# Gathers written evenly over the V part, gate loads and a weight load pinned on the load queue, one U chunk behind the first dense block's transposes

## The chip, the cores and the metric

One core of a Trainium2 chip. The metric is device microseconds (us) of one execution. Times within the execution are counted from the first instruction.

## The reference, cut to what matters

One decoder block on 512 positions of width 1024. A mixer (windowed attention beside gated linear attention) comes first; the change does not touch it. Then the channel mixer, with 16384 experts, of which each of 8 heads picks 16 per position:

```python
def block(args):
    xb, eb, gb = args
    ub = jnp.take(u, eb, axis=0)
    hid = jax.nn.gelu(jnp.einsum('tkd,td->tk', ub, xb), approximate=False) * gb
    vb = jnp.take(v, eb, axis=0)
    return jnp.einsum('tk,tkd->td', hid, vb)
...
x = x + gate2 * peer_ffn(h2, peer_wq[l], peer_subkeys[l], peer_u[l], peer_v[l])
...
return rms_norm(x, final_norm_w)
```

## The kernel before, in words

The positions are four blocks of 128. Three of them (`DENSE`, 384 positions) go through **all** experts as dense products; the fourth (`GB` = 3) gathers just the rows it picked.

*Dense path.* The experts are 128 chunks of 128. `u_part(c)` (L687) loads a pair of chunks of U (1 MB, three buffers `raw`), splits a chunk into a high part (ScalarE, L59) and a low part (VectorE or GpSimd, L60), multiplies it with the positions in 24 matmuls of 384 columns (L64 to L66), and applies GELU (ScalarE, L699). Even chunks (`AHEAD`) are computed early and stored to DRAM (`gsp`, L701); odd ones stay in SBUF. The gates of a dense block are made as one-hot products: `route(n)` (L779) finds experts and gates on VectorE in four steps, `gate_transposes(n)` (L836) transposes the two index tiles on TensorE (L841), copies them by ScalarE (L842) and splits the gates into three bf16 parts (L848 to L851), and `gate_group` (L854) builds one-hot tiles on VectorE (L862, L867), multiplies them on TensorE (L874), copies the result (L876) and writes 1 MB of gates to DRAM (`Gd`, L878), 24 times. `v_part(c)` (L1008) loads a pair of chunks of V (L1012), every eighth chunk a piece of the gates (`gr`, L1015, 12 KB a partition, two buffers), multiplies GELU by gates (L1024), splits both into high and low parts (L1028, L1029, L60), and `v_matmuls` adds 18 matmuls of 512 columns into six accumulators.

*Gather path.* `gather_u(s)` (L885) fetches 128 rows of U (0.5 MB) by an indirect DMA that GpSimd issues, and VectorE reduces them with the positions (L889); every eighth step ScalarE and VectorE make eight columns of the hidden values (L892, L893). `gather_v(s)` (L895) fetches rows of V and VectorE adds them to `gacc` (L902). All use a ring `gr` of five buffers, which the one-hot tiles `o12` use before.

*What orders the work.* The framework orders each engine's queue, and SP's queue of loads, when it builds the program: it plays the program through in a simulated run and issues on each engine what is ready, and among what is ready what was written first (`schedule_with_timeline_sim`, L38). Within the stretch from L977 to L994, VectorE and GpSimd keep the written order among the instructions written there; GpSimd does so to the end. On the chip each queue is then in order.

*Order as written.* The steps are `route(3)`, `route(0)`, the transposes of block 0, its gate groups, then blocks 1 and 2. Between steps `u_ahead` (L707) writes U parts: at step k of the first eight it has written up to `WQ_U + (ROUTE_U - WQ_U) * k // 8`, that is 12 to 19 of the 64 even chunks; the 19th is chunk 36. After these steps come the odd chunks 1, 3, 5, 7, and the V loop (L1064): for chunk c the U part of chunk c + 9 (even c), `v_part(c)`, its matmuls, then `gather_to` (L1068), which brings the gathers written so far to 8 + 2 (c + 1). The list of gathers has 18 of U, then V and U by turns. `fwb`, the last norm's weight (0.5 MB over all partitions, L1070), is written after chunk 16.

Of the kernel before, what the change touches and what calls it, by code (L numbers as in the profile page):

```python
# [1 line left out]

# [5 lines left out]
F32 = mybir.dt.float32  # L8
# [9 lines left out]
P = 128  # L18
D = 1024
KD = 8  # L20
# [8 lines left out]
TD = 128 * len(DENSE)  # L29
GB = 3  # L30
TG = 16
NGRP = TD // TG


AHEAD = tuple(range(0, P, 2))
# [6 lines left out]
def peer_block_kernel(ctx: ExitStack, tc: tile.TileContext, a: dict, out: bass.AP):  # L42
    nc = tc.nc
# [8 lines left out]
    def raw(shape, name):  # L52
        return st.tile(shape, F32, tag="raw", bufs=3, name=name)

    def hilo(src, shape, name, lo_eng):
        pool, bufs = ring["hl"]
        hi = pool.tile(shape, FR, tag="hi", bufs=bufs, name=name + "h")
        lo = pool.tile(shape, FR, tag="lo", bufs=bufs, name=name + "l")
        nc.scalar.activation(hi, src, AF.Copy)  # L59
        lo_eng.tensor_tensor(lo, src, hi, OP.subtract)  # L60
        return hi, lo

    def mm3(acc, lh, ll, rh, rl, start, stop):
        nc.tensor.matmul(acc, lh, rh, start=start, stop=False)  # L64
        nc.tensor.matmul(acc, lh, rl, start=False, stop=False)  # L65
        nc.tensor.matmul(acc, ll, rh, start=False, stop=stop)  # L66

    def bcast_load(t, src, n):
        nc.sync.dma_start(t, bass.AP(tensor=src.tensor, offset=src.offset, ap=[[0, P], [1, n]]))

    def rstd_of(pool, ss, n, w, name):
        m = pool.tile([P, w], F32, name=name + "m", tag="rsm", bufs=2)
# [21 lines left out]
    ident = cp.tile([P, P], F32, name="ident")  # L94
# [22 lines left out]
    def bank(name, tag="m"):  # L117
        return banks["pool"].tile([P, 512], F32, tag=tag, bufs=BUFS[tag], name=name)
# [4 lines left out]
    def pbank(name):  # L123
        return ps.tile([P, 512], F32, tag="ph", name=name)
# [485 lines left out]
    h2Th = h2p.tile([P, KD, T], FR, name="h2Th")  # L610
    h2Tl = h2p.tile([P, KD, T], FR, name="h2Tl")
# [72 lines left out]
    gsp = dr.tile([len(AHEAD), P, TD], F32, name="gsp")  # L684
    ges = {}

    def u_part(c, lo_eng=None):  # L687

        j = c // 2 % 2
        if j == 0:  # L690
            u_part.raw[c % 2] = raw([P, 2, KD, P], f"u{c}")
            nc.sync.dma_start(u_part.raw[c % 2], a["uT"][c // 4 + (c % 2) * (P // 4)])
        uh, ul = hilo(u_part.raw[c % 2][:, j], [P, KD, P], f"uc{c}", lo_eng or nc.vector)
        ph = ps.tile([P, 512], F32, tag="ph", name=f"ph{c}")[:, :TD]
        for k in range(KD):
            mm3(ph, uh[:, k, :], ul[:, k, :], h2Th[:, k, :TD], h2Tl[:, k, :TD], k == 0, k == KD - 1)
        ge = dnA.tile([P, NGRP, TG], F32, tag="ge", bufs=RING, name=f"ge{c}")
        gef = ge.rearrange("p g t -> p (g t)")
        nc.scalar.activation(gef, ph, AF.Gelu)  # L699
        if c % 2 == 0:  # L700
            nc.scalar.dma_start(gsp[c // 2], gef)  # L701
        else:
            ges[c] = ge

    u_part.raw = {}

    def u_ahead(upto, lo_eng=None):  # L707
        while u_ahead.n < min(upto, len(AHEAD)):
            u_part(AHEAD[u_ahead.n], lo_eng)
            u_ahead.n += 1  # L710
# [66 lines left out]
    I12 = {}  # L777
# [50 lines left out]
    CG = 8  # L828
    Gd = dr.tile([P // CG, P, NGRP, CG * TG], F32, name="Gd")
# [6 lines left out]
    def gate_transposes(n):  # L836

        t12 = rt.tile([P, P // 2, 2, 2], BF, tag="t12", bufs=2, name=f"t12{n}")
        for s in range(2):
            pt = bank(f"tr{s}{n}", BK[s])  # L840
            nc.tensor.transpose(pt[:, :P], I12[n][:, s], ident)  # L841
            nc.scalar.activation(t12[:, :, s], pt[:, :P].rearrange("p (g r) -> p g r", r=2), AF.Copy)  # L842
        pt = bank(f"trg{n}", BK[2])
        nc.tensor.transpose(pt[:, :P], gates[n], ident)
        gp3 = rt.tile([P, P // 2, 3, 2], BF, tag="gp3", bufs=2, name=f"gp3{n}")
        r = rt.tile([P, P], F32, tag="gr3", bufs=1, name=f"gr3{n}")
        pair = lambda v: v.rearrange("p (g r) -> p g r", r=2)
        nc.scalar.activation(gp3[:, :, 0], pair(pt[:, :P]), AF.Copy)  # L848
        nc.vector.tensor_tensor(pair(r), pair(pt[:, :P]), gp3[:, :, 0], OP.subtract)
        nc.scalar.activation(gp3[:, :, 1], pair(r), AF.Copy)  # L850
        nc.vector.tensor_tensor(gp3[:, :, 2], pair(r), gp3[:, :, 1], OP.subtract)  # L851
        trs[n] = t12, gp3

    def gate_group(bi, n, q):  # L854
        t12, gp3 = trs[n]
# [25 lines left out]
    NS = P  # L881
# [20 lines left out]
            nc.vector.scalar_tensor_tensor(gacc, vr, hg[:, s:s + 1], gacc, op0=OP.mult, op1=OP.add)  # L902


    EARLY, VLAG = 8, 10
    gathers = [(gather_u, s) for s in range(EARLY)]
    rest = [(s * 0.88 / (NS - EARLY), gather_u, s + EARLY) for s in range(NS - EARLY)]
    rest += [((s + VLAG) / (NS + VLAG), gather_v, s) for s in range(NS)]
    gathers += [g[1:] for g in sorted(rest, key=lambda g: g[0])]

    def gather_to(upto):
        while gather_to.n < min(upto, len(gathers)):
            f, s = gathers[gather_to.n]
            f(s)
            gather_to.n += 1
# [30 lines left out]
    WQ_U, ROUTE_U, LAST_U = 11, 19, 5  # L946
# [26 lines left out]
        steps += [lambda n=n: gate_transposes(n)] + grp[:6] + late + grp[6:]  # L973
    NSTEP = 4 * len(DENSE) + 4 + 2 * NGRP
    k = 0
    dve_s = ExitStack()
    dve_s.enter_context(tc.manual_schedule(engines={mybir.EngineType.DVE, mybir.EngineType.Pool}))  # L977
    for g in steps:
        if callable(g):
            g()  # L980
            continue
        for _ in g:
            k += 1
            if k <= 8:
                u_ahead(WQ_U + (ROUTE_U - WQ_U) * k // 8)
            else:
                u_ahead(ROUTE_U + (len(AHEAD) - LAST_U - ROUTE_U) * (k - 8) // (NSTEP - 8))
        if g is steps[0]:
            nc.vector.scalar_tensor_tensor(ix_u, I12[GB][:, 0], 128.0, I12[GB][:, 1], op0=OP.mult, op1=OP.add)
            nc.vector.scalar_tensor_tensor(ix_v, I12[GB][:, 1], 128.0, I12[GB][:, 0], op0=OP.mult, op1=OP.add)  # L990
            nc.vector.tensor_copy(gg_g, gates[GB])
# [8 lines left out]
    dn = ctx.enter_context(tc.tile_pool(name="dn", bufs=1, side="right", reuse_waits="tile"))  # L1000
    pacc = ctx.enter_context(tc.tile_pool(name="pacc", bufs=1, space=PSUM, side="right", reuse_waits="tile"))
    acc = [pacc.tile([P, 512], F32, name=f"acc{i}") for i in range(2 * len(DENSE))]
    fwb = dn.tile([P, D], F32, name="fwb")
    gacc = dn.tile([P, D], F32, name="gacc")
    vPc = a["vP"].rearrange("(c i) d -> c i d", i=P)
    LAST = 4

    def v_part(c):  # L1008
        if c % 2 == 0:

            v_part.raw = dn.tile([P, 2, D], F32, tag="vraw", bufs=2, name=f"v{c}") if c else raw([P, 2, D], "v0")
            nc.sync.dma_start(v_part.raw, vPc[c:c + 2].rearrange("c i d -> i c d"))  # L1012
        if c % CG == 0:
            v_part.g = dn.tile([P, NGRP, CG, TG], F32, tag="gring", bufs=2, name=f"gr{c}")
            nc.sync.dma_start(v_part.g.rearrange("p g c t -> p g (c t)"), Gd[c // CG])  # L1015
        vh, vl = hilo(v_part.raw[:, c % 2], [P, D], f"vc{c}", nc.vector)
        if c % 2 == 0:
            if c % 4 == 0:
                v_part.ge = dnA.tile([P, 2, TD], F32, tag="gel", bufs=2, name=f"gel{c}")
                nc.sync.dma_start(v_part.ge, gsp[c // 2:c // 2 + 2].rearrange("c p t -> p c t"))  # L1020
            ge = v_part.ge[:, c // 2 % 2].rearrange("p (g t) -> p g t", g=NGRP)
        else:
            ge = ges.pop(c)
        nc.vector.tensor_tensor(ge, ge, v_part.g[:, :, c % CG, :], OP.mult)  # L1024
        gef = ge.rearrange("p g t -> p (g t)")
        Ah = dn.tile([P, TD], FR, tag="Ah", bufs=4, name=f"Ah{c}")
        Al = dn.tile([P, TD], FR, tag="Al", bufs=4, name=f"Al{c}")
        nc.scalar.activation(Ah, gef, AF.Copy)  # L1028
        nc.vector.tensor_tensor(Al, gef, Ah, OP.subtract)  # L1029
        return c, Ah, Al, vh, vl  # L1030
# [33 lines left out]
    for c in range(P - LAST):  # L1064
        if c % 2 == 0 and c + 1 + LEAD < P:
            u_part(c + 1 + LEAD)
        v_matmuls([v_part(c)])
        gather_to(EARLY + (len(gathers) - EARLY) * (c + 1) // (P - LAST))  # L1068
        if c == 16:
            bcast_load(fwb, a["fw"], D)  # L1070
        if c == P - 16:

            dg = gp.tile([P, KD, P], F32, tag="gr", bufs=GR, name="dg")
            nc.vector.tensor_tensor(dg, ident[:, None, :].to_broadcast([P, KD, P]),
                                    modT[:, 40:48, None].to_broadcast([P, KD, P]), OP.mult)
            for q in range(2):
                pb = pbank(f"g2b{q}")
                for i in range(4):
                    nc.tensor.matmul(pb[:, i * P:(i + 1) * P], ones, dg[:, 4 * q + i, :], start=True, stop=True)
                nc.scalar.activation(h2n[:, q * 512:(q + 1) * 512], pb, AF.Copy)  # L1080
# [67 lines left out]
```

## Time and profile before

| what | value |
|---|---|
| median of 3 runs | 1559.18 us (1557.12 to 1560.58) |
| the profiled execution | 1555.13 us, its span 1553.4 us |
| granted TensorE clock, mean | 0.990 |
| TensorE busy | 1493.2 us (96%) |
| VectorE busy | 1251.8 us (81%) |
| ScalarE busy | 688.8 us (44%) |
| GpSimd busy | 412.9 us (27%) |
| loads of u, v, gr | 64 of 1024 KB, 64 of 1024 KB, 16 of 1536 KB |
| writes of Gd | 24 of 1024 KB |

The table is the average over stages. A wait is read in the rows below: the number in square brackets behind an instruction is how long its engine was idle before it, and behind the arrow stands what came last of the things that it waited for. An instruction's own time (second column) can overlap the next one's.

### The profile page before, as it was taken

To read this page: it belongs to the slowest core of one execution; us is meant where nothing else is said; L and a number is where in the kernel's file an instruction comes from. 1 tells how busy PE (TensorE), PEld (TensorE's weight loads), DVE (VectorE), ACT (ScalarE), POOL (GpSimd) and SP (SyncE) were. 2 spreads that over 40 slices of the span, in tenths; PEclk is the share of its full clock that TensorE was granted. 3 is DMA by queue.
4 is the path that set the end of the run, shared out by engine and by line. 5 is a ranking of instruction groups with operands and counts; after the bars stand their busy time and mean duration, and the time that the engine had idled before them with its cause. 6 is when DMAs were issued, how large, how long until landed. Compare 5 with 4: busy or idle time off the path is not lost.

```text
span 1553.4 us, 24408 instructions
## 1 busy us (share of the span) xinstructions
PE 1493.2 (96%) x9379; PEld 1328.2 (86%) x9379; DVE 1251.8 (81%) x2476; ACT 688.8 (44%) x1078; POOL 412.9 (27%) x327
## 2 busy tenths in 40 slices
PE   4999989899999999999999999999999999999996
PEld 3787878888998999999888888888888888888885
DVE  7578668589989898995678778878888878887997
ACT  5545576433445666564333333333333333333343
POOL 1000000144500000003243334433434434434550
PEclk9999999999999999999999999999999999999998
DMA  9253444262346677679998999888998989898893
GB/s 349 89 204 131 171 142 173 108 239 92 127 155 188 198 239 235 201 239 388 380 348 317 339 348 346 322 340 333 364 330 329 338 340 354 326 340 334 292 331 129
DMA packets 154932, 409.67 MB, mean 264 GB/s; under 512 B 10288, under 2 KB 77120, under 8 KB 142400
## 3 DMA queue, kind: packets, MB, share of 16 engines
q1 hardware_dynamic: 108736, 261.30, 47.2%
q0 software_dynamic: 36864, 134.23, 23.0%
q10 hardware_dynamic: 9216, 12.59, 2.2%
q8 instruction: 73, 1.20, 0.3%
q14 instruction: 43, 0.35, 0.1%
HBM read 366.14 MB, written 41.94 MB: 263 GB/s over the span
## 4 chain that ended last, share of the span: by engine, by line
PE 63%; DVE 3%; DMA 2%; ACT 1%; issue 1%; DVEq 0%; ACTq 0%; SPq 0%
PE acc L65 11%; PE acc L64 11%; PE acc L66 11%; PE ph L66 8%; PE ph L64 8%; PE ph L65 8%; PE pg L874 4%; DMA Gd<-gs 1%; DMA gr<-Gd 1%; DVE o L867 1%; ACT gs L876 0%; DVE o L862 0%; DVE oh L819 0%; DVE oh L822 0%; DVE oh L817 0%
## 5 line engine op out<-in xcount | busy, mean ns | idle before, releaser
L887 POOL DMA_INDIRECT gu<-in_u_dram,ix_u x128 | 170.2, 1329 | 531.5 <-PE pg L874 273.5
L897 POOL DMA_INDIRECT gv<-in_vP_dram,ix_v x128 | 171.0, 1336 | 214.9 <-DVE gu L889 183.1
L902 DVE SCALAR_TENSOR_TENSOR gacc<-gv,hg,gacc 128x1024 f32<-128x1024 f32 x127 | 162.7, 1281 | 3.3 <-DMA gv<-in_vP_dram,ix_v 3.1
L889 DVE SCALAR_TENSOR_TENSOR gu<-gu,h2n 128x1024 f32<-128x1024 f32 x128 | 156.0, 1219 | 5.9 <-DMA gu<-in_u_dram,ix_u 5.9
L1028 ACT ACTIVATE Ah<-ge 128x384 fp32r<-128x384 f32 x64 | 33.6, 525 | 155.1 <-PE acc L65 155.1
L1028 ACT ACTIVATE Ah<-gel 128x384 fp32r<-128x384 f32 x64 | 33.6, 525 | 154.4 <-PE acc L65 154.4
L876 ACT ACTIVATE gs<-pg 128x512 f32<-128x512 f32 x96 | 94.3, 1108 | 9.8 <-PE pg L874 9.8
L867 DVE TENSOR_TENSOR o<-o,gp 128x1024 bf16<-128x1024 bf16 x144 | 91.0, 687 | 4.3
L874 PE MATMUL pg<-o,o 128*128 128x128 bf16 x1152 | 79.3, 223 | 5.3 <-DVE o L867 5.3
L874 PEld LDWEIGHTS <-o 128*128 128x128 bf16 x1152 | 69.7, 99 | 14.4 <-issue 8.5
L953 POOL IOTA iot<- 128x256 bf16 x1 | 1.5, 1541 | 282.8 <-DVE h2Tl L675 282.8
L1029 DVE TENSOR_TENSOR Al<-gel,Ah 128x384 fp32r<-128x384 f32 x64 | 35.6, 556 | 45.2 <-ACT Ah L1028 45.2
L699 ACT ACTIVATE ge<-ph 128x384 f32<-128x384 f32 x128 | 60.8, 475 | 23.8 <-PE ph L66 23.7
L862 DVE TENSOR_TENSOR o<-iot,t 128x2048 bf16<-128x2048 bf16 x48 | 58.5, 1218 | 4.9 <-ACT t L842 4.9
L1029 DVE TENSOR_TENSOR Al<-ge,Ah 128x384 fp32r<-128x384 f32 x64 | 35.5, 555 | 19.2 <-ACT Ah L1028 18.1
L1024 DVE TENSOR_TENSOR ge<-ge,gr 128x384 f32<-128x384 f32 x64 | 35.4, 553 | 10.9 <-ACT ge L699 10.9
L212 DVE SCALAR_TENSOR_TENSOR macc<-wa,scs,macc 128x1024 f32<-128x1024 f32 x28 | 39.0, 1392 | 4.9 <-DMA wa<-in_w_ada_dram 4.7
L1024 DVE TENSOR_TENSOR gel<-gel,gr 128x384 f32<-128x384 f32 x64 | 32.8, 553 | 0.0
L65 PE MATMUL pq<-h2Tl,wq_0h 128*128 128x512 f32 (+1 forms) x80 | 27.9, 349 | 1.2 <-DVE h2Tl L675 1.2
L64 PE MATMUL pq<-h2Th,wq_0h 128*128 128x512 f32 (+1 forms) x80 | 28.0, 352 | 1.0 <-ACT qha L751 1.0
L65 PE MATMUL pq<-h2Tl,wq_1h 128*128 128x512 f32 (+1 forms) x80 | 28.2, 353 | 0.0
L66 PE MATMUL pq<-h2Th,wq_1l 128*128 128x512 f32 (+1 forms) x80 | 28.2, 352 | 0.0
(2599 smaller groups left out, 5077.1 us busy)
## 6 DMA issues: line engine op xcount, KB each, us to landing
u<-in_uT_dram SPq DMA_DIRECT2D x64, 1024.0 KB
v<-in_vP_dram SPq DMA_DIRECT2D x64, 1024.0 KB
Gd<-gs SPq DMA_DIRECT2D x24, 1024.0 KB
gr<-Gd SPq DMA_DIRECT2D x16, 1536.0 KB
wa<-in_w_ada_dram SPq DMA_DIRECT2D x20, 1024.0 KB
gsp<-ge ACTq DMA_DIRECT2D x64, 192.0 KB
gel<-gsp SPq DMA_DIRECT2D x32, 384.0 KB
wi<-in_w_in_dram SPq DMA_DIRECT2D x9, 1024.0 KB
```

Of the source, the lines that this page charges most:

```text
L64: nc.tensor.matmul(acc, lh, rh, start=start, stop=False)
L65: nc.tensor.matmul(acc, lh, rl, start=False, stop=False)
L66: nc.tensor.matmul(acc, ll, rh, start=False, stop=stop)
L867: nc.vector.tensor_tensor(o2[:, :, m], o12[:, :, 1], gp3[:, g0:g0 + H, m, None].to_broadcast([P, H, P, 2]), OP.mult)
L874: nc.tensor.matmul(pt[:, i, :], o12[:, g, 0, :, r], o2[:, g, m, :, r], start=(m == 0), stop=(m == 2))
L876: nc.scalar.activation(gs[:, :, t0 + 4 * f:t0 + 4 * f + 4].rearrange("p b a -> p a b"), pt, AF.Copy)
L887: nc.gpsimd.indirect_dma_start(out=ur, out_offset=None, in_=a["u"], in_offset=bass.IndirectOffsetOnAxis(ap=ix_u[:, s:s + 1], axis=0))
L889: nc.vector.scalar_tensor_tensor(ur, ur, 1.0, h2n, op0=OP.mult, op1=OP.mult, accum_out=hid[:, s:s + 1])
L897: nc.gpsimd.indirect_dma_start(out=vr, out_offset=None, in_=a["vP"], in_offset=bass.IndirectOffsetOnAxis(ap=ix_v[:, s:s + 1], axis=0))
L902: nc.vector.scalar_tensor_tensor(gacc, vr, hg[:, s:s + 1], gacc, op0=OP.mult, op1=OP.add)
L1024: nc.vector.tensor_tensor(ge, ge, v_part.g[:, :, c % CG, :], OP.mult)
L1029: nc.vector.tensor_tensor(Al, gef, Ah, OP.subtract)
```

## The change

It adds no arithmetic and takes none away. Three things move. (1) The constant `EARLY` goes: the gathers are spread evenly, 256 (c + 1) / 124 written after chunk c, and in the list 11 of U stand first. (2) `gates_of` writes the load of gate piece 0 behind the load of `v0`, and that of piece j + 1 in chunk 8j + 2; these loads and `fwb`'s are pinned: `keep_in_program_order` holds an instruction behind the one written before it on its queue. (3) In the first eight steps `u_ahead` writes up to 11 + 7k // 8 U parts, and the 19th, chunk 36, is written after block 0's transposes; `issue_after` queues its matmuls behind the second index transpose on TensorE.

```diff
-    def u_part(c, lo_eng=None):
+    def u_part(c, lo_eng=None, after=None):
...
-        for k in range(KD):
-            mm3(ph, uh[:, k, :], ul[:, k, :], h2Th[:, k, :TD], h2Tl[:, k, :TD], k == 0, k == KD - 1)
+        with tc.issue_after(after.ins) if after is not None else nullcontext():
+            for k in range(KD):
+                end = mm3(ph, uh[:, k, :], ul[:, k, :], h2Th[:, k, :TD], h2Tl[:, k, :TD], k == 0, k == KD - 1)
...
-            nc.tensor.transpose(pt[:, :P], I12[n][:, s], ident)
+            tr = nc.tensor.transpose(pt[:, :P], I12[n][:, s], ident)
...
-    EARLY, VLAG = 8, 10
-    gathers = [(gather_u, s) for s in range(EARLY)]
-    rest = [(s * 0.88 / (NS - EARLY), gather_u, s + EARLY) for s in range(NS - EARLY)]
-    rest += [((s + VLAG) / (NS + VLAG), gather_v, s) for s in range(NS)]
-    gathers += [g[1:] for g in sorted(rest, key=lambda g: g[0])]
+    VLAG = 10
+    gathers = [(s * 0.88 / NS, gather_u, s) for s in range(NS)]
+    gathers += [((s + VLAG) / (NS + VLAG), gather_v, s) for s in range(NS)]
+    gathers = [g[1:] for g in sorted(gathers, key=lambda g: g[0])]
...
         if callable(g):
-            g()
+            tr = g()
+            if first is None:
+
+                first = u_part(AHEAD[u_ahead.n], after=tr)
+                u_ahead.n += 1
             continue
...
-                u_ahead(WQ_U + (ROUTE_U - WQ_U) * k // 8)
+                u_ahead(WQ_U + (ROUTE_U - 1 - WQ_U) * k // 8)
...
+    def gates_of(j):
+        gates_of.next = dn.tile([P, NGRP, CG, TG], F32, tag="gring", bufs=2, name=f"gr{j}")
+        tc.keep_in_program_order(
+            nc.sync.dma_start(gates_of.next.rearrange("p g c t -> p g (c t)"), Gd[j]))
+
...
+        if c == 0:
+            gates_of(0)
         if c % CG == 0:
-            v_part.g = dn.tile([P, NGRP, CG, TG], F32, tag="gring", bufs=2, name=f"gr{c}")
-            nc.sync.dma_start(v_part.g.rearrange("p g c t -> p g (c t)"), Gd[c // CG])
+            v_part.g = gates_of.next
+        if c % CG == 2 and c + CG < P:
+            gates_of(c // CG + 1)
...
-        gather_to(EARLY + (len(gathers) - EARLY) * (c + 1) // (P - LAST))
+        gather_to(len(gathers) * (c + 1) // (P - LAST))
         if c == 16:
-            bcast_load(fwb, a["fw"], D)
+            tc.keep_in_program_order(bcast_load(fwb, a["fw"], D))
```

## Rows read from the trace of the kernel before

**Rows 1.** Stages: PE, PEld, DVE, ACT, POOL busy (instructions), PEclk, DMA share, GB/s

```profile
470.00:510.00 40.00, 39.77 (x356) 38.21 (x355) 39.10 (x48) 24.91 (x29) 0.00 (x0) 0.94 0.66 203
...
710.00:780.00 70.00, 65.27 (x349) 61.82 (x347) 42.28 (x65) 24.75 (x38) 20.01 (x16) 0.95 0.99 394
...
1200.00:1460.00 260.00, 260.00 (x1256) 228.91 (x1256) 213.55 (x276) 92.80 (x131) 106.75 (x83) 1.00 0.89 333
```

**Rows 2.** Timeline of TensorE: start us, us, engine line op out<-in xcount [idle<-releaser]

```profile
460.62 0.33 PE L64 MATMUL ph<-h2Th,uc36h 128*128 128x384 f32 x1
...
464.61 0.34 PE L66 MATMUL ph<-h2Th,uc36l 128*128 128x384 f32 x1
464.78 0.38 PE L841 MATMUL tr<-ident,I 128*128 128x128 f32 x2
...
468.61 0.37 PE L874 MATMUL pg<-o,o 128*128 128x128 bf16 x2 [1.70 <-DVE o L867]
```

**Rows 3.** Timeline of ScalarE around the transposes

```profile
460.64 1.06 ACT L59 ACTIVATE uc42h<-u 128x1024 fp32r<-128x1024 f32 x1 [2.72 <-PE ph L65]
...
461.98 0.30 ACT L850 ACTIVATE gp<-gr 128x128 bf16<-128x128 f32 x1
...
466.14 0.27 ACT L842 ACTIVATE t<-tr 128x128 bf16<-128x128 f32 x1
```

**Rows 4.** Timeline of VectorE, from block 0's softmax to its first one-hot tile

```profile
443.55 0.40 DVE L787 TENSOR_REDUCE zz<-g 128x8 f32<-128x128 f32 x1 [0.38 <-ACT g L786]
...
444.43 1.22 DVE L60 TENSOR_TENSOR uc30l<-u,uc30h 128x1024 fp32r<-128x1024 f32 x1
...
462.31 0.29 DVE L851 TENSOR_TENSOR gp<-gr,gp 128x128 bf16<-128x128 f32 x1 [2.59 <-ACT gp L850]
...
466.61 1.22 DVE L862 TENSOR_TENSOR o<-iot,t 128x2048 bf16<-128x2048 bf16 x1 [4.00 <-ACT t L842]
```

**Rows 5.** Slices of TensorE: us, PE busy (instructions), PEclk, DMA share, GB/s

```profile
468.00:472.00 4.00, 2.93 (x25) 0.54 0.00 0
472.00:476.00 4.00, 3.77 (x31) 0.61 0.22 45
```

**Rows 6.** Timeline of TensorE from the U part to the V part

```profile
738.75 0.69 PE L64 MATMUL ph<-h2Th,uc1h 128*128 128x384 f32 x1 [2.76 <-ACT ge L699]
...
746.12 0.45 PE L64 MATMUL ph<-h2Th,uc3h 128*128 128x384 f32 x1 [0.17 <-ACT ge L699]
...
764.58 1.65 PE L64 MATMUL acc<-vc0h,Ah 128*128 128x512 f32 x6 [1.52 <-ACT vc0h L59]
766.51 0.50 PE L65 MATMUL acc<-vc0l,Ah 128*128 128x512 f32 x1 [0.28 <-DVE vc0l L60]
```

**Rows 7.** A slice within it, columns as in the stages

```profile
740.00:744.00 4.00, 4.00 (x14) 4.00 (x13) 1.86 (x4) 0.00 (x0) 2.62 (x2) 0.50 1.00 411
```

**Rows 8.** Timeline of ScalarE from the U part to the V part

```profile
737.26 1.06 ACT L59 ACTIVATE uc5h<-u 128x1024 fp32r<-128x1024 f32 x1 [8.20 <-DMA u<-in_uT_dram]
...
744.62 1.06 ACT L59 ACTIVATE uc7h<-u 128x1024 fp32r<-128x1024 f32 x1 [5.93 <-DMA gr<-Gd]
...
763.09 0.49 ACT L699 ACTIVATE ge<-ph 128x384 f32<-128x384 f32 x1 [3.67 <-PE ph L66]
763.48 1.05 ACT L59 ACTIVATE vc0h<-v 128x1024 fp32r<-128x1024 f32 x1
```

**Rows 9.** Timeline of SP's queue of loads: start us, us to issue, what

```profile
713.08 14.39 SPq L692 DMA_DIRECT2D u<-in_uT_dram  x1
...
737.63 0.42 SPq L69 DMA_DIRECT2D fwb<-in_fw_dram  x1
```

**Rows 10.** The chain of waits: start us, us, what

```profile
734.30 9.87 DMA gr<-Gd
744.25 0.33 ACTq L701
```

**Rows 11.** GpSimd's U gathers (L887) alone: stretch, us, busy (count), PEclk, DMA share, GB/s

```profile
690.00:764.00 74.00, 21.61 (x17) 0.95 1.03 387
```

More of the change, by code (lines that the diff above doesn't have):

```diff
@@ L1 @@
-from contextlib import ExitStack
+from contextlib import ExitStack, nullcontext
 import concourse.bass as bass
@@ L65, in mm3 @@
         nc.tensor.matmul(acc, lh, rl, start=False, stop=False)
-        nc.tensor.matmul(acc, ll, rh, start=False, stop=stop)
+        return nc.tensor.matmul(acc, ll, rh, start=False, stop=stop)
     def bcast_load(t, src, n):
-        nc.sync.dma_start(t, bass.AP(tensor=src.tensor, offset=src.offset, ap=[[0, P], [1, n]]))
+        return nc.sync.dma_start(t, bass.AP(tensor=src.tensor, offset=src.offset, ap=[[0, P], [1, n]]))
     def rstd_of(pool, ss, n, w, name):
@@ L703, in u_part @@
             ges[c] = ge
+        return end
     u_part.raw = {}
@@ L852, in gate_transposes @@
         trs[n] = t12, gp3
+        return tr
     def gate_group(bi, n, q):
@@ L975, in peer_block_kernel @@
     k = 0
+    first = None
     dve_s = ExitStack()
```

## The prediction, made blind

> **What bounds the kernel now.** I read the stage table first. From 1200 to 1460 us, deep in the V part, TensorE is busy for 260.00 of 260 us at full clock [rows 1]: nothing done to loads, gathers or VectorE there can gain, and they can only lose. Two stages stand out against that: 470 to 510, with a granted clock of 0.94, and 710 to 780, with 65.27 of 70 us busy, clock 0.95 and a DMA share of 0.99 [rows 1]. The change touches both places, so the sum is made there.
>
> *First place, the start of the first dense block.* TensorE finishes chunk 36's U products at 464.78, and only then runs the two index transposes [rows 2]. ScalarE copies them out at 466.14 [rows 3]. VectorE, which has nothing to do for 4.00 us, starts the first one-hot tile at 466.61 [rows 4], and TensorE, idle for 1.70 us, starts on the first gate products at 468.61 [rows 2]. The clock falls behind that: 0.54 and 0.61 in the two slices from 468 to 476 [rows 5].
>
> *Second place, the passage from the U part to the V part.* TensorE waits 2.76 us for chunk 1's accumulator, runs that chunk's 24 products at half clock (0.50 in 740 to 744), waits 1.52 us for chunk 0's V operand and 0.28 us for its low part [rows 6, 7]. The first wait goes back through ScalarE: chunk 5's high part stands in its queue until 737.26, when its load lands, and the GELU that frees the accumulator stands behind it [rows 8]. That load's issue held SP for 14.39 us [rows 9]. After it the first gate load leaves at 734.30 and takes 9.87 us; the chain goes from its landing to a gsp store on ScalarE's own queue [rows 10], behind which chunk 7's high part has waited 5.93 us [rows 8].
>
> **The change, part by part.**
>
> *1. Chunk 36's U products behind the transposes.* Removed: 24 products ahead of the transposes. They took from 460.62 to 464.78, that is 4.16 us for 24 products, whose first and last are shown [rows 2]. Work moved is 4.16 us, so the gain here cannot exceed 4.2 us. Nothing is added, but eight U parts (chunks 22 to 36) each move one route step later on VectorE, whose order is by hand here.
>
> Whom that makes late: chunk 28's low part now stands behind the softmax of block 0 instead of ahead of it in the tail of route(3). That softmax waits for ScalarE's exponential, so its reduction stays near 443.2 to 443.6 instead of moving up by a whole 1.14 us, and the low part that stood after it started at 444.43 [rows 4]. I get 444.05 for the start and 445.25 for the end. TensorE reaches chunk 28 at 443.8 (four U parts of 4.16 us before 460.62, and some 0.2 us for a transpose among them) and has two products without the low part, 0.35 us: a stall of 1.1 us. The six other low parts up to chunk 34 come out 0.3 to 1.5 us ahead of TensorE by the same count. Their four 1 MB loads have three raw buffers, two pairs of chunks, ahead of use: a step (about 3.5 us) later costs nothing while that cover holds, and up to that step if it is gone.
>
> What is gained: uc42h follows chunk 34's end, now 461.7 instead of 460.64. From there to the second gate copy's end ScalarE took 1.64 us (460.64 to 462.28 [rows 3]), and the two index copies add 0.44 us. The first one-hot can start at 463.8 instead of 466.61: **2.8 us** earlier, which is what VectorE, pacing this stretch, gains. The other end: chunk 36's low part is now written behind the second VectorE step of the transposes, which waited 2.59 us for the gate copy and ran at 462.31 [rows 4]. If ScalarE keeps that order, the low part is ready at 464.85 (1.1 + 462.31 + 0.29, and 1.14), while TensorE has work (transposes, two products) to 462.4: it idles 2.4 us, the clock falls again, and the 1.1 us of stall may be all that is left, as a loss. So -1.1 to 4.2; I take 2.8, since ScalarE's rows give it directly. Nothing in the later blocks changes, and TensorE-bound work carries what is gained to the end.
>
> *2. No gathers ahead (EARLY gone).* Already in the kernel before, no gather is written ahead of chunk 0's V products: the first call stands behind them. Yet 17 are issued by 764 [rows 11]. The planner issues what is ready; fwb, written behind chunk 16, leaves at 737.63 too [rows 9]. Fewer gathers in the early calls do not make any less ready. The number of gathers is the same (256), only 11 instead of 18 U rows now stand ahead of the first V row on POOL's queue, and later ones rank lower against chunks 1 to 4. I cost it at nothing: a gather's VectorE step is about 1.2 us, and the slack that hides eight of them is the V part, where TensorE never waits [rows 1]. Were that cover gone, eight times 1.2 us, 9.8 us, is the most it could cost.
>
> *3. The loads on SP.* gr 0 (1.5 MB) moves behind the load of v0 (1 MB), gr 1 behind v2, gr j+1 behind that of chunk 8j+2, fwb (0.5 MB) behind v16. No instruction is added. Later gate loads have 6 chunks of about 6.2 us in hand and a free buffer by then, so they no longer hold SP; they hid already, so nothing. In the passage the gain is that v0, no longer stuck on SP behind gr 0's wait for Gd, is early in the plan as well, so that its high part is not planned behind chunk 9's GELU: ScalarE sat idle before that GELU, and ran vc0h straight after it at 763.48 [rows 8], so an earlier place costs nothing. That takes away 1.52 and 0.28, **1.8 us** [rows 6]. Bounds: the whole passage costs 2.76 + 0.17 + 1.52 + 0.28 idle and 7.20 - 4.16 = 3.04 us for chunk 1 at half clock, so at most 7.8 gained; on the other side 6.0 lost (the slower rival). I take 1.8, as rows put a cause of order, not of traffic, on just these two waits.
>
> Here a rule weighs in. The rows show gr 0 taking 9.87 us [rows 10], with a U load issued up to 727.47 ahead of it on SP's queue [rows 9]. The Trainium skill, "DMA: Bandwidth & Descriptors", section "Queues, rings and completion order", says that each DMA engine takes turns between queues and works through one queue's ring in order; by that v0 ahead of gr 0 delays the gate load by the whole of v0, which speaks against this pin, and the sum would be the slower rival's instead of mine.
>
> **The sum.** 2.8 + 1.8 = 4.6 us. The profiled execution took 1555.13 us (its span 1553.4), so 1550.5 by its measure; it lies 4.05 us under the median of the runs, 1559.18, and against that median the forecast is **1554.6 us**. A measurement of this kernel can tell about 0.2% from no change, 3.1 us.
>
> **The rivals.**
>
> *The gathers do stay behind* (the change does what its words say). Traffic in 710 to 780 falls from a share of 0.99, chunk 5's load lands in time, and the passage's 7.8 us go with the 2.8: 1559.18 - 10.6 = 1548.6. For it: gathers move 17 rows of 0.5 MB in that stretch, about 8.9 MB. Against: readiness, not program order, decided before. 0.16.
>
> *Nothing to be measured.* The U products shift one wait into another (stall of 1.1 us, ScalarE's order kept, clock falls again), so that about 0.8 us are left, and vc0h keeps its place: 1558.4. For it: VectorE needs the same time for its steps, and two of the three edits move work under a TensorE that is busy anyway. 0.28.
>
> *Slower: the gate load behind v0.* The place is ScalarE's queue at 744: the gsp store waits for gr 0, then chunk 7's high part, the GELU and chunk 3's products. It decides as soon as gr 0 lands later than now, since chunk 1's products end at 745.95 and chunk 3's start at 746.12 [rows 6]. v0 is 1.05 MB; at the passage's 394 GB/s [rows 1] that is 2.7 us, at gr 0's own pace (two thirds of 9.87) 6.6 us. I price it at 4.6, plus 3.0 us of a second spell of half clock, less the 2.8 of part 1, 1.8 not gained: 1559.18 + 4.8 = 1564.0. Against: which store waits for which load depends on the planner's count, and may fall on another load. 0.14.
>
> **How the numbers follow.** The forecast has 0.42. Its own range is 1553.2 (4.2 + 1.8) to 1558.5 (-1.1 + 1.8). The range for 8 in 10 reaches to the first rival below, with a little for its parts, and into the slower one above without its upper half: 1547.5 to 1563. Faster by over 0.2% means under 1556.1: all of the first rival, 0.35 of the forecast's 0.42 and 0.01 of the second, 0.52. Slower: 0.14 and 0.01 for parts that add up badly, 0.15. The rest, 0.33, is the same.
>
> **What would show it.** Part 1: the transposes right behind chunk 34's products, the first one-hot about 3 us earlier against chunk 34's end, a wait of about 1 us at chunk 28, and a clock over 0.9 in the slices after. Part 2: still some 10 or more gathers issued before the first V product; no more than five would mean that the first rival holds. Part 3: v0 ahead of gr 0 on SP, fwb behind v16, vc0h ahead of chunk 9's GELU, no wait at the first V product. I am wrong if the 2.76 us wait and the half clock at chunk 1 vanish, or if chunk 3's products wait for a gate load.

## The result, and the profile after

| kernel | median | runs | range |
|---|---|---|---|
| before, same chip | 1557.07 us | 6 | 1554.99 to 1560.58 |
| changed | 1547.21 us | 6 | 1545.03 to 1554.58 |

The ratio is 0.9941, with a 95% interval from 0.9919 to 0.9962: about 9.2 us faster, where 4.6 were forecast. The changed kernel's profiled execution took 1545.37 us (span 1543.6); 9.76 us lie between it and the one of before.

**The first dense block.** The first two stages of [rows 1], a slice of [rows 5] and that of [rows 7] in the changed kernel:

```profile
470.00:510.00 40.00, 40.00 (x359) 38.64 (x357) 38.73 (x49) 25.61 (x30) 0.00 (x0) 1.00 0.78 241
710.00:780.00 70.00, 68.64 (x371) 65.07 (x371) 44.71 (x61) 25.04 (x37) 18.62 (x16) 1.00 0.98 383
...
472.00:476.00 4.00, 4.00 (x41) 3.84 (x40) 3.90 (x6) 1.83 (x3) 0.00 (x0) 1.00 0.99 342
740.00:744.00 4.00, 4.00 (x25) 4.00 (x24) 2.37 (x3) 1.51 (x3) 1.62 (x2) 1.00 1.05 425
```

Both stages with a clock under 1 are at 1.00 now, and the DMA share of the passage is 0.98, where it was 0.99. TensorE's timeline, to be held against [rows 2]:

```profile
444.55 0.44 PE L66 MATMUL ph<-h2Th,uc28l 128*128 128x384 f32 x1 [0.80 <-DVE uc28l L60]
...
460.98 0.38 PE L843 MATMUL tr<-ident,I 128*128 128x128 f32 x2
461.12 0.42 PE L64 MATMUL ph<-h2Th,uc36h 128*128 128x384 f32 x1
...
465.19 0.33 PE L66 MATMUL ph<-h2Th,uc36l 128*128 128x384 f32 x1
...
465.71 1.62 PE L877 MATMUL pg<-o,o 128*128 128x128 bf16 x24
```

ScalarE and VectorE in the same stretch, against [rows 3, 4]:

```profile
458.68 0.32 ACT L852 ACTIVATE gp<-gr 128x128 bf16<-128x128 f32 x1 [0.40 <-DVE gr L851]
461.00 1.06 ACT L59 ACTIVATE uc42h<-u 128x1024 fp32r<-128x1024 f32 x1 [2.00 <-PE ph L65]
...
462.33 0.27 ACT L844 ACTIVATE t<-tr 128x128 bf16<-128x128 f32 x1
```

```profile
459.03 0.29 DVE L853 TENSOR_TENSOR gp<-gr,gp 128x128 bf16<-128x128 f32 x1 [0.46 <-ACT gp L852]
459.24 1.22 DVE L60 TENSOR_TENSOR uc36l<-u,uc36h 128x1024 fp32r<-128x1024 f32 x1
462.80 1.23 DVE L865 TENSOR_TENSOR o<-iot,t 128x2048 bf16<-128x2048 bf16 x1 [2.35 <-ACT t L844]
```

The transposes stand ahead of chunk 36, the stall at chunk 28 is there (0.80 us; 1.1 forecast), and TensorE goes from chunk 36 to gate products without the 1.70 us wait. The copy that I feared behind uc42h ran ahead of it.

**The passage.** TensorE, then ScalarE, then SP's queue, against [rows 6, 8, 9]:

```profile
733.89 0.44 PE L64 MATMUL ph<-h2Th,uc1h 128*128 128x384 f32 x1 [1.36 <-ACT ge L700]
...
759.22 0.39 PE L64 MATMUL acc<-vc0h,Ah 128*128 128x512 f32 x1
```

```profile
732.41 1.06 ACT L59 ACTIVATE uc5h<-u 128x1024 fp32r<-128x1024 f32 x1 [6.80 <-PE ph L65]
...
736.82 1.06 ACT L59 ACTIVATE uc7h<-u 128x1024 fp32r<-128x1024 f32 x1 [2.98 <-DMA u<-in_uT_dram]
...
739.58 1.06 ACT L59 ACTIVATE uc9h<-u 128x1024 fp32r<-128x1024 f32 x1 [1.32 <-DMA v<-in_vP_dram]
...
748.28 1.06 ACT L59 ACTIVATE vc0h<-v 128x1024 fp32r<-128x1024 f32 x1 [0.85 <-DMA v<-in_vP_dram]
```

```profile
709.80 11.77 SPq L692 DMA_DIRECT2D u<-in_uT_dram  x1
...
723.10 1.52 SPq L1024 DMA_DIRECT2D v<-in_vP_dram  x2
...
732.40 0.37 SPq L1024 DMA_DIRECT2D v<-in_vP_dram  x1
732.87 0.90 SPq L1018 DMA_DIRECT2D gr<-Gd  x2
```

One wait is left. SP sends v2 and v4 at 723.10, right behind the U loads, then v0 at 732.40 and both gate pieces; in the kernel before it stood for 6.2 us (728.08 to 734.27) waiting for the last write of Gd, and all V loads left after that. vc0h runs 11 us ahead of its first use. What I had not forecast is chunk 7's high part: 736.82, not 744.62, and behind a U load, not behind gr 0. GpSimd issues as many gathers up to 764 as before, 19 for 17, 15 of them of U against [rows 11]:

```profile
690.00:764.00 74.00, 20.00 (x15) 1.00 1.03 395
```

**Where the 9.8 us are.** From the starts of the same products in both timelines: 0.76 us ahead of chunk 28 (0.5 of it already at 150 us, where nothing was changed); 4.03 from chunk 28 to chunk 44 (42.38 us before, 38.35 after); 1.55 given back between chunks 80 and 100, where the changed kernel's profile has a spell of half clock; 6.79 from the end of chunk 126 to TensorE's end (805.59 to 798.80); 0.47 given back behind TensorE's end; the rest of the way differs by 0.2.

### The profile page after: what moved, and what is told of

The parts are those of the page before. It is cut to its first block, busy times and chain, and to the rows that moved or that the text cites. A ratio compares the mean times of both kernels' runs of the same rounds, so it can differ in the third digit from the quotient of the medians.

```text
span 1543.6 us, 24413 instructions
## 1 busy us (share of the span) xinstructions
PE 1488.5 (96%) x9379; PEld 1324.5 (86%) x9379; DVE 1250.4 (81%) x2476; ACT 688.4 (45%) x1078; POOL 407.3 (26%) x327
## 4 chain that ended last, share of the span: by engine, by line
PE 65%; DVE 3%; ACT 1%; issue 0%; DMA 0%; DVEq 0%; ACTq 0%
PE acc L65 11%; PE acc L64 11%; PE acc L66 11%; PE ph L64 9%; PE ph L66 9%; PE ph L65 9%; PE pg L877 4%; DVE o L870 1%; ACT gs L879 0%; DVE oh L821 0%; DVE o L865 0%; DVE oh L819 0%; DMA u<-in_uT_dram 0%; DVE y L1063 0%; DVE y L1073 0%
## 5 line engine op out<-in xcount | busy, mean ns | idle before, releaser
L900 POOL DMA_INDIRECT gv<-in_vP_dram,ix_v x128 | 164.7, 1287 | 255.1 <-DVE gu L892 196.8
```

Of the source, the lines that this page charges most:

```text
L900: nc.gpsimd.indirect_dma_start(out=vr, out_offset=None, in_=a["vP"], in_offset=bass.IndirectOffsetOnAxis(ap=ix_v[:, s:s + 1], axis=0))
```

## The experiments

Each kernel was run against the kernel before in five rounds. Intervals are 95%; microseconds are the ratio's distance from 1 times 1557.

### One edit at a time

The U edit alone (`u_part(..., after=tr)`, `ROUTE_U - 1 - WQ_U`):

> Before with the U edit alone. My theory: the first dense block gives 4.8 us, as the changed kernel's trace shows at its second block (first one-hot products 536.38 to 531.58), and the passage to the V part stays as before (waits of 2.76 and 1.52 us, chunk 1 at half clock), since it has its own cause there: 0.9970, that is -4.7 us. Rival (the passage's waits were only a matter of when TensorE arrives): the passage improves too, -8 us or more. Rival (nothing in the first block holds to the end): within 1.5 us of before.

0.9980 [0.9969, 0.9992], 3.1 us faster. From chunk 28 to chunk 44 its profile takes 38.32 us. The passage is not better; from the end of chunk 126 to TensorE's end it takes 1.3 us more than before, with half clock from 747.4 on:

```profile
738.72 0.45 PE L64 MATMUL ph<-h2Th,uc1h 128*128 128x384 f32 x1 [2.27 <-ACT ge L700]
...
746.25 0.44 PE L64 MATMUL ph<-h2Th,uc3h 128*128 128x384 f32 x1 [3.10 <-ACT ge L700]
```

The pins of the gate loads and of `fwb` alone (`gates_of`, two `keep_in_program_order`):

> Before with the gate loads and fwb pinned, U part and gathers as before. My theory: the wait of 1.52 and 0.28 us at the first V product goes (-1.8), and if the 2.76 us wait at chunk 1 shrinks below what lets the clock fall, 3.0 to 4.4 us more: -1.8 to -6.4 us. Rival (the gathers did it): within 1.5 us of before, waits in the passage as before. Slower rival: gr 0 lands later behind v0 and chunk 3's products wait for it: +2.6 to +6.

0.9956 [0.9944, 0.9968], 6.9 us faster, more than the forecast for the whole change. Its passage has one wait, at chunk 1; its first block has the 42 us of before, less a shorter spell of half clock (41.40).

```profile
736.04 0.44 PE L64 MATMUL ph<-h2Th,uc1h 128*128 128x384 f32 x1 [1.71 <-ACT ge L699]
```

The gathers alone (no `EARLY`):

> Before with EARLY gone alone. My theory: readiness decides, some 17 gathers are still issued before the first V product, and the time is within 1.5 us of before. Rival (the gathers did it): fewer than 10 issued by then, DMA share under 0.9 in 710 to 780, -5 to -8 us.

1.0004 [0.9993, 1.0015]: nothing, and 17 gathers up to 764 as before. The three edits add up: 3.1 and 6.9 faster, 0.6 slower make 9.4, and all together measured 9.2. The passage with the gathers alone:

```profile
737.17 0.65 PE L64 MATMUL ph<-h2Th,uc1h 128*128 128x384 f32 x1 [2.24 <-ACT ge L699]
...
744.71 0.44 PE L64 MATMUL ph<-h2Th,uc3h 128*128 128x384 f32 x1 [1.52 <-ACT ge L699]
```

The passages of the U edit and of the gathers tell something that the one of before hid [rows 6]. There chunk 1 ran at half clock and chunk 3 waited for 0.17 us; here chunk 1 runs at full clock, or half of it does, and chunk 3 waits for 3.10 or 1.52. Counted from the end of chunk 126, chunk 3 starts at 10.13 us (before), 9.81 and 9.78. Something other than the clock holds chunk 3: chunk 7's high part, behind gr 0.

### The gathers kept out of the passage

The changed kernel, with the first gather held back:

```diff
-        v_matmuls([v_part(c)])
+        end = v_matmuls([v_part(c)])
+        if c == 0:
+            gather_to.after = end
...
+        if s == 0:
+            tc.add_manual_dep(ins.ins, gather_to.after.ins.name, ...)
```

> The changed kernel with the first gather made to wait for chunk 0's last V product, so that really none runs ahead. What the words of the change promise: DMA share in 700 to 740 falls well under 1, the wait of 1.35 us at chunk 1 goes, up to -1.4 us against the changed kernel and no more, because nothing else is left in the passage; against before 0.993. Rival (18 gathers less ahead cost VectorE time in the V part that it does not have): gathers end later, the last blocks wait for VectorE, slower than the changed kernel by up to 18 x 1.2 = 22 us, less what slack takes; -9.8 + 22 against before at worst.

0.9986 [0.9975, 0.9996], some 7 us slower than the changed kernel. The passage does come clear: no wait at chunk 1, a DMA share of 0.79 from 690 to 764. But the gathers miss at the end. TensorE ends at 1530.85, the last row of V is added then, and the last norm follows behind it (VectorE's timeline):

```profile
1529.17 1.28 DVE L908 SCALAR_TENSOR_TENSOR gacc<-gv,hg,gacc 128x1024 f32<-128x1024 f32 x1 [2.83 <-DMA gv<-in_vP_dram,ix_v]
1530.49 1.29 DVE L1066 TENSOR_TENSOR y<-gacc,h2n 128x512 f32<-128x512 f32 x2
```

In the changed kernel the second of these steps, the first of the gather path's norm, runs at 1519.35, 12 us ahead of TensorE's end. From chunk 126 to TensorE's end the held-back kernel takes 798.4 us, the changed one 798.8; from there to the end of the span 22.9 and 12.3. So the gathers in the passage cost the wait of 1.36 us at chunk 1, of which 0.4 us is left at TensorE's end, and buy the end.

### Which pin, and why

My theory after the first four runs was that the gate loads' place did all of it.

> The kernel before with the gate loads moved and pinned, and fwb left as it was. Theory (the place of the gate loads on SP does all of it): the 6.9 us of both pins, ratio about 0.9956; in the passage one wait of 1.3 to 1.8 us at chunk 1, none at chunk 3, none at the first V product, and the store on ScalarE's queue behind chunk 1's GELU no longer waits for gr 0. Rival (fwb's 0.5 MB, sent among the loads of the passage, is what delays them): less than half of it, 3.4 us or less, and the waits at chunk 3 stay in part.

> The kernel before with fwb's load alone pinned behind chunk 16. Theory: nothing, 1.000 within 0.001; fwb is issued behind gr 0 and v0 in the kernel before, and chunk 5's and chunk 7's loads are on the way by then. Rival (fwb's traffic counts): 3.4 us or more faster.

It fell. Gate loads alone: 0.9986 [0.9974, 0.9998], 2.2 us. `fwb` alone: 0.9957 [0.9942, 0.9971], 6.7 us, though up to the first V product it takes one load of 0.5 MB from SP's queue, behind gr 0, and changes no other order. ScalarE's timeline, with the gate pins alone and then with `fwb`'s alone:

```profile
742.13 1.06 ACT L59 ACTIVATE uc7h<-u 128x1024 fp32r<-128x1024 f32 x1 [5.35 <-DMA v<-in_vP_dram]
```

```profile
742.67 1.06 ACT L59 ACTIVATE uc7h<-u 128x1024 fp32r<-128x1024 f32 x1 [2.54 <-DMA u<-in_uT_dram]
...
746.38 1.06 ACT L59 ACTIVATE uc9h<-u 128x1024 fp32r<-128x1024 f32 x1 [2.27 <-DMA gr<-Gd]
```

Chunk 7's high part, behind the store of chunk 124's GELU, waits for gr 0 before [rows 8], for a V load with the gate pins, for a U load with `fwb`'s pin, where the wait for gr 0 has gone one store further, ahead of chunk 9. None of these is data that the instruction reads. The traces show what it is, by the counter (a semaphore) that each DMA counts up as it lands: the 363 DMAs of SP and ScalarE share eight counters in turn, 45 or 46 each, over both queues, and a DMA waits until the one that had its counter before has landed. In the kernel before, gr 0 lands at 744.17, and the store of chunk 124's GELU, on the same counter, leaves at 744.25. With the gate pins alone that counter was v2's (landed 741.68, the store leaves at 741.76); with `fwb`'s pin it was that of chunk 9's U load (742.22 and 742.29). gr 0 is eight places ahead of chunk 124's store in the kernel before; without `fwb` between them it is eight ahead of chunk 126's, and chunk 9's U load is eight ahead of chunk 124's. With the gate pins alone TensorE still waits at chunk 3:

```profile
743.62 0.69 PE L64 MATMUL ph<-h2Th,uc3h 128*128 128x384 f32 x1 [2.34 <-ACT ge L699]
```

Two more kernels ask the same. In the first, gate piece 0 is written ahead of v0, both pins kept:

> Both pins, but gate piece 0 pinned ahead of v0 in place of behind it. Theory (what counts is that SP sends v0 and v2 while it would wait for the last write of Gd): SP stands at gr 0 until about 734 us again, v0 comes late and a store on ScalarE's queue waits for gr 0 or for v0: 5 to 7 us of the 6.9 are given back, ratio 0.999 to 1.000. Rival (any pin of the gate loads does it, because later gate pieces and fwb leave the passage): the 6.9 us stay, ratio about 0.9956.

0.9980 [0.9968, 0.9992], between the two: 3.8 of the 6.9 us are given back. `fwb` is out of the passage, so chunk 3 does not wait; v0 leaves last (738.18 and after) and its wait is back:

```profile
739.73 0.44 PE L64 MATMUL ph<-h2Th,uc1h 128*128 128x384 f32 x1 [2.11 <-ACT ge L699]
...
762.52 0.74 PE L64 MATMUL acc<-vc0h,Ah 128*128 128x512 f32 x2 [1.70 <-ACT vc0h L59]
```

In the second, the kernel before with three stores moved to SP's queue:

```diff
-            nc.scalar.dma_start(gsp[c // 2], gef)
+            (nc.scalar if c < 122 else nc.sync).dma_start(gsp[c // 2], gef)
```

> The kernel before with the last three gsp stores (chunks 122 to 126) issued by SP in place of ScalarE; no other order changes. Theory (chunk 3's products wait because a gsp store on ScalarE's queue waits for gr 0): chunk 7's high part runs when its load is there, about 739 in place of 744.62, and no wait is left at chunk 3: 1.5 to 3.1 us faster in executions without half clock at chunk 1, and 0.2 us in those with it, so 0 to 3 us in the median; the waits at chunk 1 (2.2 to 2.8) and at the first V product (1.5 and 0.3) stay. Rival (chunk 7's high part really waits for its own load, and the store's wait is beside it): no change, chunk 7's high part still near 744.

0.9984 [0.9972, 0.9995], 2.5 us. Chunk 7's high part no longer waits for any store, and TensorE's wait at chunk 3 is gone; the wait at chunk 1 is shorter than expected (1.20) and that at the first V product longer (2.87, not 1.5 and 0.3):

```profile
736.37 1.05 ACT L59 ACTIVATE uc7h<-u 128x1024 fp32r<-128x1024 f32 x1
```

```profile
760.46 1.42 PE L64 MATMUL acc<-vc0h,Ah 128*128 128x512 f32 x5 [2.87 <-ACT vc0h L59]
```

### Places or traffic

One kernel adds a place without traffic (the pin holds `fwb` right behind the small load; both leave where `fwb` did), one takes the stores out of play but leaves `fwb`'s traffic.

```diff
-            bcast_load(fwb, a["fw"], D)
+            bcast_load(dn.tile([P, 8], F32, name="few"), a["fw"], 8)
+            tc.keep_in_program_order(bcast_load(fwb, a["fw"], D))
```

> The kernel before with one load of 4 KB (eight words to each partition) put ahead of fwb's load on SP, and nothing else; order and traffic of the passage stay. Theory (a store that ScalarE issues waits for the DMA that was issued eight places before it, counted over both queues, whatever that was): everything behind fwb moves one place, so the store of chunk 122's GELU, ahead of chunk 5's high part, waits for chunk 9's U load, and v0's load on SP waits for gr 0. Chunk 5's high part then runs at 739 to 742 in place of 737.26, the wait at chunk 1 grows from 2.2 to 2.8 us to 4 or more, and v0 leaves SP at about 744 in place of 740.53, so that the wait at the first V product grows as well: 2 to 6 us slower, ratio 1.0013 to 1.004. Rival (traffic counts, not places): 4 KB change nothing, 1.000 within 0.001, and chunk 5's high part waits for its own load as before.

1.0071 [1.0054, 1.0088]: 11 us slower from a load of 4 KB. The passage did what was expected, the wait at the first V product apart, which stayed at 1.53:

```profile
740.65 1.06 ACT L59 ACTIVATE uc5h<-u 128x1024 fp32r<-128x1024 f32 x1 [10.72 <-DMA u<-in_uT_dram]
```

```profile
742.14 0.69 PE L64 MATMUL ph<-h2Th,uc1h 128*128 128x384 f32 x1 [5.28 <-ACT ge L699]
...
767.13 1.20 PE L64 MATMUL acc<-vc0h,Ah 128*128 128x512 f32 x4 [1.53 <-ACT vc0h L59]
```

By the first V product that is 1.7 us (it starts 30.27 us behind chunk 126's end, 28.59 before). The rest is spread over the whole V part. One stretch of it in this kernel, and below it in the next one:

```profile
1180.00:1280.00 100.00, 100.00 (x478) 86.88 (x478) 80.39 (x105) 34.64 (x50) 41.06 (x31) 1.00 0.89 335
```

```profile
1180.00:1280.00 100.00, 100.00 (x484) 88.07 (x483) 81.19 (x105) 36.08 (x51) 42.66 (x33) 1.00 0.91 340
```

478 products in 100 us, for 484. The next kernel differs by the size of the tile alone (`dn.tile([P, 1024], ...)[:, :8]`):

> The run with one more load of 4 KB again, but the tile that it fills takes 4096 bytes of each partition in place of 32; the order of every queue is that of that run. There the wait at chunk 1 grew to 5.28 us as expected, but the time grew by 11 us, and most of that lay in the V part, whose products came 0.235 us apart in place of 0.229. Theory (the 32 bytes moved the V part's tiles in SBUF, and that is a cost of its own; the places in the queues cost what the passage shows): V products 0.229 us apart again, the wait at chunk 1 still 4 us or more with half clock behind it, and 1.5 to 3.5 us slower than the kernel before, ratio 1.0010 to 1.0023. Rival (the later v0 and gr 0 leave the V part short of data all along): still 0.235 us apart and 1.006 to 1.008.

1.0004 [0.9992, 1.0016]. The V part is at its old pace, so its loss came with the 32-byte tile and not with the load. The wait at chunk 1 stays:

```profile
743.19 0.69 PE L64 MATMUL ph<-h2Th,uc1h 128*128 128x384 f32 x1 [4.67 <-ACT ge L699]
...
768.52 0.73 PE L64 MATMUL acc<-vc0h,Ah 128*128 128x512 f32 x2 [1.52 <-ACT vc0h L59]
```

The time measured, 0.6 us slower, is under the 1.5 to 3.5 expected, and its interval (1.2 faster to 2.5 slower) holds both nothing and the 1.4 us of its profile. So a place alone, without traffic, moves the wait, which the rows show; its price is within the measurement.

The gate pins, with the three stores on SP and `fwb` left in the passage:

> The kernel before with the gate loads pinned as in the change, fwb left in the passage, and the last three gsp stores issued by SP. Theory (fwb's pin gains only because it moves ScalarE's stores to other predecessors): with the stores off ScalarE's queue the gate pins give the whole of what both pins gave, ratio about 0.9956 (-6.9 us, as an interval -4.5 to -7.5); one wait of about 1.2 us at chunk 1, none at chunk 3, none at the first V product, though fwb is still issued near 731. Rival (fwb's 0.5 MB themselves hold up the U loads): no more than the 2.2 us of the gate pins alone or the 2.5 us of the stores alone, 3.5 us at most.

0.9972 [0.9960, 0.9985], 4.4 us: just short of the theory's 4.5 to 7.5, and over the rival's 3.5. The passage is as expected, one wait of 0.99 us, and from chunk 126 to TensorE's end the kernel takes as long as the one with both pins (799.1 and 799.0), though `fwb` is in the passage. What it lacks against that one lies elsewhere: 1.2 us behind TensorE's end, and in its profile the longer spell of half clock in the first block (6.8 us, for 3.4):

```profile
737.96 0.44 PE L64 MATMUL ph<-h2Th,uc1h 128*128 128x384 f32 x1 [0.99 <-ACT ge L699]
```

The table sets the kernels side by side, from TensorE's timelines, but for the one with the 32-byte tile, whose loss lies in the V part: its wait at chunk 1; the start of chunk 5's products, counted from the end of chunk 126; the wait at the first V product; from the end of chunk 126 to TensorE's end; and from there to the end of the span (all in us).

| kernel | chunk 1 | chunk 5 | first V | to TensorE's end | behind it | measured |
|---|---|---|---|---|---|---|
| before | 2.76 | 14.42 | 1.52 + 0.28 | 805.6 | 11.8 | |
| U edit | 2.27 | 15.65 | 1.52 + 0.27 | 806.8 | 11.8 | -3.1 |
| gathers | 2.24 | 14.07 | 1.52 + 0.28 | 805.3 | 11.7 | +0.6 |
| 4 KB more, wide tile | 4.67 | 15.82 | 1.52 + 0.28 | 807.0 | 11.8 | +0.6 |
| gate pins | 0.91 | 13.52 | none | 803.1 | 13.5 | -2.2 |
| stores on SP | 1.20 | 9.63 | 2.87 | 801.6 | 11.8 | -2.5 |
| both pins, gate 0 first | 2.11 | 10.56 | 1.70 | 801.7 | 11.8 | -3.1 |
| `fwb`'s pin | 1.89 | 10.32 | 1.83 | 801.5 | 9.6 | -6.7 |
| gate pins, stores on SP | 0.99 | 9.43 | none | 799.1 | 13.5 | -4.4 |
| both pins | 1.71 | 10.28 | none | 799.0 | 12.3 | -6.9 |
| changed | 1.36 | 10.04 | none | 798.8 | 12.3 | -9.2 |

Two effects add up. Where a store holds chunk 7 until gr 0 or a V load lands (with 4 KB more: chunk 5 until chunk 9's load lands), chunk 5 starts 13.5 us or later, else at 9.4 to 10.6: some 4 us to TensorE's end. And the gate pins take away the wait at the first V product: some 2.5 us more. The time behind TensorE's end differs by up to 3.9 us between these kernels; it is part of why `fwb`'s pin alone measures as well as both (9.6 against 12.3). The planner orders the end anew in each. With `fwb`'s pin VectorE multiplies block 0 by the last norm's weight ahead of TensorE's end (1539.78); before, behind it (1541.58), among the last block's steps. VectorE before, then with `fwb`'s pin:

```profile
1542.22 1.41 DVE L1058 SCALAR_TENSOR_TENSOR y<-y,rf0y,fwb 128x512 f32<-128x512 f32 x2
...
1548.67 1.41 DVE L1058 SCALAR_TENSOR_TENSOR y<-y,rf2y,fwb 128x512 f32<-128x512 f32 x2
```

```profile
1538.97 1.42 DVE L1058 SCALAR_TENSOR_TENSOR y<-y,rf0y,fwb 128x512 f32<-128x512 f32 x2
...
1544.75 1.41 DVE L1058 SCALAR_TENSOR_TENSOR y<-y,rf2y,fwb 128x512 f32<-128x512 f32 x2
```

The last block's multiplication starts 7.1 us behind TensorE's end before and 5.0 with the pin, which is the 2.1 us. Why the planner orders it so was not followed further.

### A version beyond the change

A chunk's U products behind the transposes of all three dense blocks:

```diff
-            if first is None:
-                first = u_part(AHEAD[u_ahead.n], after=tr)
-                u_ahead.n += 1
+            u_part(AHEAD[u_ahead.n], after=tr)
+            u_ahead.n += 1
```

> The changed kernel with a chunk's U products behind the transposes of the second and third dense block as well. Theory (the first block gained because VectorE sat idle for 4.00 us there; at the later blocks VectorE is busy for 19.7 of 20 us and sets the pace): nothing, 0.9941 against the kernel before within 0.0015. Rival (TensorE's wait of 1.45 us and the half clock behind it at 615 us, together about 3.1 us, come from the transposes standing behind U products there too): 1.5 to 3 us faster than the changed kernel, 0.992 to 0.993.

0.9920 [0.9903, 0.9937], median 1545.59 us, the lowest of all. The value is the rival's, but its interval overlaps the change's, so a gain over it is not shown, and the rival's reason is not borne out: the wait is still there, 1.46 us up to 621.41. What this profile lacks is the half clock behind it and the wait at chunk 1.

## Why the prediction was right, and where it was wrong

*Part 1, the U products.* Right in mechanism and size. Forecast 2.8 us within -1.1 to 4.2; from chunk 28 to chunk 44 the timelines give 3.1 us against a kernel with 3.4 us of half clock there (41.40) and 4.0 against the one before with 6.8 (42.38), and the edit alone measures 3.1. The first one-hot tile comes 19.73 us behind chunk 28's start, 22.78 before. The rival in which ScalarE keeps its order did not come about.

*Part 2, the gathers.* Right: nothing, as 1.0004 shows, and as many issued. The rival in which they stay behind was made by hand, on the changed kernel: its wait of 1.36 us at chunk 1 goes, 0.4 us of it is left at TensorE's end, and the end loses 10.6. What it would do to the passage of the kernel before, the 7.8 us of the rival, was not tried.

*Part 3, the loads.* This is the step that failed. Its own term held: the wait at the first V product went, and the gate pins alone measured 2.2 for 1.8. What it left out is a third wait. It took 1.8 us, "as rows put a cause of order, not of traffic, on just these two waits". The same rows put a cause of order on a third: chunk 7's high part, 5.93 us behind gr 0 [rows 8]. I read that wait as one that could only grow, in the slower rival, and named its condition without following it: that which store waits for which load depends on the planner's count. The count changed, as it does with any load added to or taken from the queues, and here the store fell on an earlier load. Nor did I see it in TensorE's rows: I booked chunk 1's 3.04 us to the clock and chunk 3's wait at 0.17, where the U edit alone and the gathers alone show that at full clock chunk 3 waits instead. In place of 1.8, the two pins measured 6.9, of which the profiles place 6.5 between chunk 126 and TensorE's end. The sign that I named against myself came half true: the half clock at chunk 1 is gone, and 1.36 of the 2.76 us of wait are left. The 6.0 us set as the worst loss do not follow from the rival that they name (4.6 and 3.0 make 7.6).

*The edit costed with the others, `fwb`.* Its place was taken to be free, because the load is hidden. The load is; its place in the count was not.

*The slower rival* did not come about: no product of TensorE waits for gr 0 in the changed kernel. gr 0 does land later there, 20.3 us behind its issue, with v2, v4 and v0 ahead of it; it was 9.87 before. The rule of the Trainium skill that spoke against the pin ("DMA: Bandwidth & Descriptors", "Queues, rings and completion order") agrees with that, but it was not put to the test by a wait. With gate 0 ahead of v0 it was v0 that came late.

*The total.* 1547.2 lies 0.3 us under the range's lower end and on the forecast's side of no change. The kernel before took 1557.07 beside it, where the forecast started from 1559.18; the ratio of 0.9941 on that base is 1550.0, inside the range. That the range reached so far is luck: its lower end was set for the rival with 0.16, and the gain came by another way than that rival's, as the DMA share of the passage did not fall.

## What to carry to other kernels

When a wait stands behind a DMA that the waiting instruction doesn't read, look for what the two share (here a counter that comes round every eight transfers, over two queues): any load added or taken away ahead of it moves the wait to another, for better or worse, so a pin is priced by what every store and load behind it will then wait for. Don't book half clock or a short wait to its own cause until an execution without it shows what else was holding the same instruction. And a queue that works ahead in a crowded stretch may be what keeps the end short: hold it back only after looking at who finishes last.

## What the runs showed of the hardware

*The size of a tile that no product reads changed the pace of TensorE.* The same program, with a tile of 32 bytes a partition in place of 4096, ran 478 in place of 484 products in 100 us of the V part, at clock 1.00 in both. V products came 0.2334 us apart on the mean, in place of 0.2290, and in every chunk alike (the 0.235 of the expectation above is from six products); over 128 chunks of 18 products that is the 10 us. From TensorE's timeline with the small tile (three products apart), and in the kernel before (18 apart):

```profile
906.92 0.39 PE L64 MATMUL acc<-vc22h,Ah 128*128 128x512 f32 x1
...
907.62 0.39 PE L64 MATMUL acc<-vc22h,Ah 128*128 128x512 f32 x1
```

```profile
901.94 0.39 PE L64 MATMUL acc<-vc22h,Ah 128*128 128x512 f32 x1
...
906.06 0.39 PE L64 MATMUL acc<-vc23h,Ah 128*128 128x512 f32 x1
```

The cause is argued, not shown: of a V product's operands the parts of GELU times gates (`Ah`, `Al`) share the pool `dn` with the tile and may be moved by its 32 bytes, while the parts of V lie in another pool (`hl`). The lost time lies around the product of the two high parts (0.237 us from the product before it, 0.226 with the wide tile; 0.232 to the one behind it, for 0.229). No run moved an operand alone.

*Half clock does not follow a wait by its length alone.* Behind the passage's first wait it came after 2.76, 4.67 and 5.28 us, and after one of 2.24, but not after 2.27 or 2.11. In the changed kernel it came after a wait of 1.45 us up to 616.45 (two slices, clock 1.00 and 0.57), which the kernel before (1.45 us up to 621.28) and the version beyond the change have too, without it:

```profile
615.00:618.00 3.00, 1.22 (x12) 0.95 (x13) 2.97 (x5) 0.95 (x2) 0.00 (x0) 1.00 0.19 69
618.00:622.00 4.00, 4.00 (x26) 4.00 (x24) 3.97 (x6) 2.14 (x2) 0.00 (x0) 0.57 0.00 0
```
